# Two-layer hybrid encoder on one core: two raw weight chunks of the MLP's lead land in the tiles of the shared sums, one pair's squares are held back in both layers, and one hold is kept in one layer only

## The chip, the core and the metric

The kernel runs on one core of one Trainium2 chip. The metric is the time of one execution in microseconds (us), and less is better. Before the change three runs took 1929.17, 1929.80 and 1929.84 us, so the median is 1929.8 us. One further execution was recorded by the hardware profiler.

## The reference

A trunk of two layers over 256 tokens of width 2048. Each layer has a token mixer (neighbourhood attention in layer 0, grouped-query attention in layer 1) beside four cross-attention heads, an output projection, and a dense MLP with squared ReLU. What matters here is the end of the projection and the MLP behind it:

```
for i in range(DEPTH):                      # DEPTH = 2
    n = rms_norm(h, attn_norm[i])
    ...
    h = h + jnp.concatenate([mix, cross], axis=-1) @ w_o[i]
    n = rms_norm(h, mlp_norm[i])
    h = h + jnp.square(jax.nn.relu(n @ w_up[i])) @ w_down[i]
return rms_norm(h, final_norm)
```

`w_up[i]` is 2048 x 8192 and `w_down[i]` is 8192 x 2048, all in float32.

## The kernel before

**Products of split numbers.** Every float32 operand is split into a high part (a copy rounded to `float32r`, on ACT) and a low part (the number less its high part, on DVE); TensorE multiplies high by high, low by high and high by low. The helper `split` (L401 on ACT, L402 on DVE) does this for every 1 MB chunk of weights. So each chunk goes: a DMA issued by SP, an ACT copy, a DVE subtraction, and then the matmuls. Names ending in `h` and `l` are the parts: `uh`, `ul` of an up chunk, `bh`, `bl` and `th`, `tl` of a down chunk.

**The MLP.** One layer has 64 up chunks, numbered m (128 features each), and a down projection that is mostly a Strassen form of seven products instead of eight over pairs of up chunks. The first six up chunks (`LEAD`) run alone, and are called the lead here; then come 58 steps, numbered n. A step is: "first" (9 matmuls with `bh`/`bl`, lines L1103, L1105, L1106), one up chunk m = 6 + n (32 matmuls, L294 and L297, in two halves), and "second" (12 matmuls with `th`/`tl`, same lines as "first"). What remains is done by plain products. `squared` (from L1004) takes the sums of an up chunk out of PSUM (`u_y`, L1012 and L1013), applies ReLU and square (`c`, L1014 and L1015), and after every second chunk makes the seven left-hand matrices of that pair (DVE, L1023 to L1025) and splits them (`a_s`). Pair j is needed first by a "first" of step n = 2, 3, ... in an order given by `RUNS`; pair 2 (chunks 4 and 5, the last of the lead) is first used in step n = 2.

**Where the raw weights land.** An up chunk's raw weights land in one of two buffers (tag `U`, function `loaded`). The third and fourth up chunk (m = 2 and m = 3) thus wait until the splits of chunk 0 and chunk 1 have been made. The two tiles `z0` and `z1` (each 128 x 2048 float32, 1 MB) hold the four shared sums of the Strassen form; they are made at the beginning of the MLP, and their first write comes at the end of step n = 3. They belong to a pool (`mlp`) that takes the memory of the pools of the projection, which are closed at that point.

**Order.** Work is cut into grains in the order of TensorE. `run_all` walks the grains and calls each grain's load, preparation and run a number of grains ahead (the triple `ahead`); `later(n, fn)` puts off a function by n grains; a scheduler then places the instructions on each engine's queue, in which they run strictly in order. `past(fn, pair)` holds the instructions of `fn` behind the pair of instructions given (an ACT copy and a DVE subtraction). In both layers the splits of chunk m = 0 are held in this way behind the last split of the projection's weights (`box["weights"]`).

Of the kernel before, what the change touches and what calls it, by code (L numbers as in the profile page):

```python
# [38 lines left out]
LEAD = 6  # L39
# [66 lines left out]
def encoder_kernel(ctx: ExitStack, tc: tile.TileContext, t: dict, out: bass.AP):  # L106
    nc = tc.nc
# [58 lines left out]
    soon = {}  # L166
# [787 lines left out]
    def up_grains(layer, m):  # L954
        own = {}
        lead = m < LEAD

        def load():
            own["raw"] = loaded(t[f"w_up{layer}"][m], "U")

        def prep(hf):

            if m == 0:
                past(lambda: prepared(hf), box["weights"])
                return
            with tc.issue_after(box["summed"].ins) if m in (1, 2) else nullcontext():
                prepared(hf)

        def prepared(hf):
            half = 2 * m + hf  # L970
            if lead and (half in (2, 4) or half > 4 and half % 3 == 2):

                if half < 5:
                    room = at.side.tile([P, 2, HALF], F32R, tag="b", bufs=3, name="u_b")
                    own[hf] = room[:, 0], room[:, 1]
                else:
                    own[hf] = tuple(at.mlp.tile([P, CH], F32R, tag=x, name=f"u_{x}")[:, :HALF] for x in ("th", "tl"))
                box["splits"].append(split(*own[hf], own["raw"][:, hf * HALF : (hf + 1) * HALF]))
            else:
                own[hf] = half_of_side(own["raw"], hf)  # L980

        def run(hf):
            if m == hf == 0:
                closed("cat", "ring")
                at.mlp = opened("mlp")
                box["z"] = [at.mlp.tile([P, 4, 512], F32, tag=f"z{q}", name=f"z{q}") for q in range(2)]
                box["z_set"], box["back"] = set(), set()
            if hf == 0:
                if lead:
                    own["ps"] = at.acc.tile([P, 512], F32, tag="acc", name="ps_u")  # L990
                else:
                    own["ps"] = sum_of("up")

            with tc.issue_after(box["late"].ins) if m == hf == 0 else nullcontext():
                products_of_both(own["ps"], box["hT"], hf * (KT // 2), KT // 2, *own.pop(hf), keep_order=not lead)

        def after():
            squared(layer, m, own["ps"])

        soon = (8, 8, 3) if m == 1 else SOONER  # L1000
        return [Grain(lambda: run(0), None, load, None, lambda: prep(0), soon),
                Grain(lambda: run(1), after, None, None, lambda: prep(1), SOONER)]

    def squared(layer, m, ps):  # L1004

        e = m % 2
        if e == 0:
            box["c"] = at.mlp.tile([P, 8, P], F32, tag="c", bufs=2, name="c")
        c = box["c"]
        two = c[:, 2 * e : 2 * e + 2, :]  # L1010
        y = at.side.tile([P, SEQ], F32, tag="junk", bufs=1, name="u_y")
        nc.scalar.activation(y, ps[:, SEQ:], AF.Copy)  # L1012
        nc.vector.tensor_tensor(y, ps[:, :SEQ], y, op=ALU.add)  # L1013
        nc.scalar.activation(two, y.rearrange("p (i b) -> p b i", b=2), AF.Relu)  # L1014
        nc.scalar.activation(two, two, AF.Square)  # L1015
        if e == 0:
            return
        pair = m // 2
        if pair >= max(STEPPED):
            a = at.mlp.tile([P, 2, 4, P], F32R, tag="a", bufs=6, name="a_p")  # L1020
            split(a[:, 0], a[:, 1], c[:, :4])
        else:
            nc.vector.tensor_tensor(c[:, 4, :], c[:, 0, :], c[:, 2, :], op=ALU.subtract)  # L1023
            nc.vector.tensor_tensor(c[:, 5:7, :], c[:, 0:5:4, :], c[:, 1, None, :].to_broadcast([P, 2, P]), op=ALU.add)
            box["made"] = nc.vector.tensor_tensor(c[:, 7, :], c[:, 3, :], c[:, 6, :], op=ALU.subtract)  # L1025
            a = at.mlp.tile([P, 2, 7, P], F32R, tag="a", bufs=6, name="a_s")
            split(a[:, 0], a[:, 1], c[:, 1:])
            if pair >= min(STEPPED):

                n = pair - min(STEPPED)  # L1030
                if n == 0:
                    box["a_0"] = at.mlp.tile([P, max(STEPPED) - min(STEPPED), 2, P], F32R, tag="a", bufs=6, name="a_0")
                split(box["a_0"][:, n, 0], box["a_0"][:, n, 1], c[:, 0])
        box["a", pair] = a
        if m == UPS - 1 and layer == 1:
            later(2, load_gf)
# [11 lines left out]
    def down_grains(layer, n, begins, ends, sooner):  # L1048

        q, j = STEPS[n]  # L1050
        own = {}

        def load():
            own["b"] = at.side.tile([P, 4, 512], F32, tag="b", bufs=3, name="b")
            nc.sync.dma_start(own["b"].rearrange("p a b -> p (a b)"),
                              t[f"w_pair{layer}"][j * 2 + q])

        def behind(fn, far=4):

            return (lambda: past(fn, box["splits"][-far])) if n < 2 else fn  # L1060

        def pre():

            b, s = own["b"], at.side.tile([P, 4, 512], F32, tag="T", bufs=2, name="t")
            nc.scalar.activation(s[:, 3, :], b[:, 3, :], AF.Copy)  # L1065
            nc.gpsimd.dma_start(s[:, 3, :], b[:, 1, :], accum_op=ALU.add)  # L1066

            with ExitStack() as held:
                if n == 2:
                    held.enter_context(tc.issue_after(box["made"].ins))  # L1070
                if 0 < n < 4:
                    held.enter_context(tc.issue_after(box["bl"].ins))
                box["t3"] = nc.vector.tensor_tensor(s[:, 0, :], b[:, 3, :], b[:, 0, :], op=ALU.add)
            nc.vector.tensor_tensor(s[:, 1, :], s[:, 0, :], b[:, 1, :], op=ALU.add)
            nc.vector.tensor_tensor(s[:, 2, :], s[:, 1, :], b[:, 2, :], op=ALU.add)
            own["t"] = s

        def prep_first():
            own["first"] = tuple(at.mlp.tile([P, 3 * 512], F32R, tag=x, name=x) for x in ("bh", "bl"))
            b = own["b"][:, :3].rearrange("p a b -> p (a b)")  # L1080
            if sooner:

                with tc.issue_after(box["t3"].ins):
                    split(*own["first"], b)
            else:
                box["bl"] = split(*own["first"], b)[1]

        def prep_second():
            own["second"] = tuple(at.mlp.tile([P, CH], F32R, tag=x, name=x) for x in ("th", "tl"))
            split(*own["second"], own["t"].rearrange("p a b -> p (a b)"))  # L1090

        def run(which, products):
            if n == 0 and which == "first":
                open_strassen(layer)
            hi, lo = own.pop(which)
            a = box["a", j]
            for name, ai, bi in products:
                if begins and name not in box["back"]:
                    sum_of(name)
                start = begins and name not in box["back"]  # L1100
                ps = pairs(box["ps"][name])
                mh, ml = (in_turn(x[:, bi * 512 : (bi + 1) * 512]) for x in (hi, lo))
                ins = nc.tensor.matmul(ps, a[:, 0, ai, :], mh, start=start, stop=False, skip_group_check=True)  # L1103
                pin(ins)
                nc.tensor.matmul(ps, a[:, 0, ai, :], ml, start=False, stop=False, skip_group_check=True)  # L1105
                nc.tensor.matmul(ps, a[:, 1, ai, :], mh, start=False, stop=ends, skip_group_check=True)  # L1106
                if begins:
                    box["back"].discard(name)

        def after(products):  # L1110
            if ends:
                for name, _, _ in products:
                    taken(q, name, n == len(STEPS) - 1)

        def after_second():
            after(SECOND)
            if ends:
                box["z_set"].add(q)
            if ends and j == STEPPED[q] - 1:
                folded(q, n == len(STEPS) - 1)  # L1120

        return [Grain(lambda: run("first", FIRST), lambda: after(FIRST), load, behind(pre), behind(prep_first, 4 if n else 1),
                      (12, 8, 4) if sooner else (12, 5, 4)),
                Grain(lambda: run("second", SECOND), after_second, None, None, behind(prep_second), SOONER)]
# [541 lines left out]
```

## Time and profile before

| | before |
|---|---|
| median of three runs | 1929.8 us (1929.17 to 1929.84) |
| the profiled execution's own time | 1932.01 us |
| its span | 1930.2 us |
| mean granted TensorE clock | 0.996 |
| HBM read | 397.78 MB |

The profile is one execution. The engines are PE (matmuls), PEld (weight loads of PE), DVE, ACT, POOL and SP; SP issues nearly all of the DMAs. A row of the timeline gives the start, the duration, the engine, the line, the operation, the tile written and the tiles read, and in brackets how long the engine sat idle before it and what ended the wait. Layer 0's projection ends and its lead begins at about 403 us; in layer 1 this is at about 1285.6 us. The loop of 58 steps follows each of them.

### The profile page before, as it was taken

The page shows a single profiled execution, that of the slowest core. Times are in us where ns is not written, and L with a number is a line of the kernel's source. Part 1 is how long each engine was busy: PE and PEld are TensorE (multiplying, and loading weights), DVE is VectorE, ACT ScalarE, POOL GpSimd, SP SyncE. Part 2 cuts the span into 40 slices and gives each one's busy share as a digit, 9 for nine tenths or more (in the row PEclk, how much of TensorE's full clock was granted, in tenths as well). Part 3 has the DMA queues.
Part 4 walks back from the last instruction along what each step waited for, and adds up shares of the span by engine and source line. Part 5 has one row for each costly group of instructions (what it writes and reads, how often), then busy time and mean ns, then how long its engine had stood idle before and what let it go on. Part 6 is the DMA issues. An engine that isn't in the chain of part 4 may idle for free.

```text
span 1930.2 us, 27774 instructions
## 1 busy us (share of the span) xinstructions
PE 1904.5 (99%) x10278; PEld 1702.3 (88%) x10278; DVE 1740.6 (90%) x2226; ACT 1406.8 (73%) x2042; POOL 153.8 (8%) x191
## 2 busy tenths in 40 slices
PE   9999999999999999999999999999999999999998
PEld 9999989888888988888888888888888888888887
DVE  7888878589999999999999778888999999999997
ACT  6755555567787887878876658667777878878785
POOL 0000000000000000000011001000000000000010
PEclk9999999999999999999999999999999999999999
DMA  8965666666877888778777765667778788788784
GB/s 301 331 209 179 228 205 201 241 214 219 247 243 245 244 247 245 232 243 246 238 241 224 262 217 166 222 213 238 244 235 250 235 244 249 232 248 243 239 251 145
DMA packets 119048, 451.35 MB, mean 234 GB/s; under 512 B 24832, under 2 KB 50176, under 8 KB 71552
## 3 DMA queue, kind: packets, MB, share of 16 engines
q1 hardware_dynamic: 99168, 415.12, 62.9%
q0 software_dynamic: 19456, 33.93, 10.8%
q8 instruction: 81, 1.33, 0.3%
q10 hardware_dynamic: 288, 0.52, 0.1%
q14 instruction: 55, 0.45, 0.1%
HBM read 397.78 MB, written 4.19 MB: 208 GB/s over the span
## 4 chain that ended last, share of the span: by engine, by line
PE 83%; DVE 7%; DMA 4%; ACT 3%; issue 2%; SPq 1%; POOL 0%; DVEq 0%; POOLq 0%; ACTq 0%
PE ps_u L297 21%; PE ps_u L294 10%; PE p L1105 9%; PE p L1106 9%; PE p L1103 9%; PE ps_s L297 5%; PE ps_m L278 5%; PE ps_m L281 5%; PE ps_m L282 5%; PE ps_s L294 3%; DVE lo L402 1%; DMA raw_U<-in_w_up 1%; PE ps_s L307 1%; SPq L503 1%; DVE ul L402 1%
## 5 line engine op out<-in xcount | busy, mean ns | idle before, releaser
L297 PE MATMUL ps_u<-hT,uh 128*128 128x512 f32 x1968 | 651.4, 382 | 0.0
L294 PE MATMUL ps_u<-hT,ul 128*128 128x256 f32 x1968 | 537.1, 273 | 1.8 <-DVE ul L402 1.8
L297 PEld LDWEIGHTS ps_u<-hT,uh 128*128 128x128 f32 x1968 | 371.8, 189 | 51.4
L294 PEld LDWEIGHTS ps_u<-hT,ul 128*128 128x128 f32 x1968 | 377.6, 192 | 7.8 <-DVE ul L402 2.6
L402 DVE TENSOR_TENSOR ul<-raw_U,uh 128x1024 fp32r<-128x1024 f32 x262 | 318.3, 1217 | 10.8 <-ACT uh L401 10.7
L402 DVE TENSOR_TENSOR lo<-raw,hi 128x1024 fp32r<-128x1024 f32 (+1 forms) x220 | 260.2, 1193 | 53.6 <-ACT hi L401 53.2
L401 ACT ACTIVATE uh<-raw_U 128x1024 fp32r<-128x1024 f32 x262 | 276.4, 1056 | 22.1 <-PE ps_u L297 9.4
L402 DVE TENSOR_TENSOR tl<-t,th 128x2048 fp32r<-128x2048 f32 x116 | 265.4, 2288 | 29.3 <-ACT th L401 28.0
L401 ACT ACTIVATE hi<-raw 128x1024 fp32r<-128x1024 f32 (+1 forms) x220 | 225.0, 1034 | 84.1 <-PE ps_m L282 58.8
L401 ACT ACTIVATE th<-t 128x2048 fp32r<-128x2048 f32 x116 | 221.5, 1910 | 38.4 <-PE p L1106 38.4
L402 DVE TENSOR_TENSOR bl<-b,bh 128x1536 fp32r<-128x1536 f32 x116 | 203.1, 1751 | 0.9 <-ACT bh L401 0.9
L1066 POOL DMA_DIRECT2D t<-b x116 | 101.1, 871 | 1072.8 <-ACT t L1065 835.8
L1103 PE MATMUL p<-th,a_s 128*128 128x512 f32 x464 | 175.9, 379 | 0.0
L1105 PE MATMUL p<-tl,a_s 128*128 128x512 f32 x464 | 175.9, 379 | 0.0
L1106 PE MATMUL p<-th,a_s 128*128 128x512 f32 x464 | 175.9, 379 | 0.0
L401 ACT ACTIVATE bh<-b 128x1536 fp32r<-128x1536 f32 x116 | 172.1, 1483 | 0.0
L297 PE MATMUL ps_s<-nT,hi 128*128 128x512 f32 x448 | 148.6, 382 | 0.0
L1105 PE MATMUL p<-bl,a_s 128*128 128x512 f32 x348 | 133.4, 383 | 2.6 <-DVE bl L402 2.6
L1103 PE MATMUL p<-bh,a_s 128*128 128x512 f32 x348 | 133.1, 383 | 2.9 <-ACT bh L401 2.9
L1106 PE MATMUL p<-bh,a_s 128*128 128x512 f32 x348 | 133.2, 383 | 0.0
L1014 ACT ACTIVATE c<-u_y 128x256 f32<-128x256 f32 x128 | 67.3, 526 | 85.3 <-DVE u_y L1013 85.3
L294 PE MATMUL ps_s<-nT,lo 128*128 128x256 f32 x448 | 122.6, 274 | 0.0
(308 smaller groups left out, 3688.5 us busy)
## 6 DMA issues: line engine op xcount, KB each, us to landing
raw_U<-in_w_up SPq DMA_DIRECT2D x128, 1024.0 KB, 6.0
b<-in_w_pair SPq DMA_DIRECT2D x116, 1024.0 KB, 6.1
raw<-in_w_o SPq DMA_DIRECT2D x32, 1024.0 KB, 5.2
t<-b POOLq DMA_DIRECT2D x116, 256.0 KB, 7.0
raw<-in_w_b SPq DMA_DIRECT2D x21, 1024.0 KB, 5.5
raw<-in_w_av SPq DMA_DIRECT2D x12, 1024.0 KB, 5.2
raw<-in_w_aq SPq DMA_DIRECT2D x12, 1024.0 KB, 5.0
raw<-in_w_ak SPq DMA_DIRECT2D x12, 1024.0 KB, 5.0
```

What stands on the lines that cost most here:

```text
L278: first = nc.tensor.matmul(ps, ah, mh, start=st, stop=False)
L281: nc.tensor.matmul(ps, ah, ml, start=False, stop=False)
L282: final = nc.tensor.matmul(ps, al, mh, start=False, stop=sp)
L294: ins = nc.tensor.matmul(pairs(ps[:, :SEQ]), lo[:, s], x[:, 0], start=k == 0, stop=False, skip_group_check=True)
L297: nc.tensor.matmul(ps.rearrange("p (n i b) -> p n i b", n=2, b=2), hi[:, s], x, start=False, stop=k == KT - 1, skip_group_check=True)
L401: first = nc.scalar.activation(dst_hi, src, AF.Copy)
L402: return first, nc.vector.tensor_tensor(dst_lo, src, dst_hi.bitcast(F32), op=ALU.subtract)
L1014: nc.scalar.activation(two, y.rearrange("p (i b) -> p b i", b=2), AF.Relu)
L1066: nc.gpsimd.dma_start(s[:, 3, :], b[:, 1, :], accum_op=ALU.add)
L1103: ins = nc.tensor.matmul(ps, a[:, 0, ai, :], mh, start=start, stop=False, skip_group_check=True)
L1105: nc.tensor.matmul(ps, a[:, 0, ai, :], ml, start=False, stop=False, skip_group_check=True)
L1106: nc.tensor.matmul(ps, a[:, 1, ai, :], mh, start=False, stop=ends, skip_group_check=True)
```

## The change

Three edits, all in the MLP's code:

1. The raw weights of up chunks m = 2 and m = 3 land in `z0` and `z1` instead of the two `U` buffers. Their load is called one grain after the grain that makes those tiles. The `U` buffers so go to chunks 0, 1, 4, 5, 6, ...
2. The hold of chunk 0's splits behind the projection's last weight split stays in layer 1 and goes in layer 0.
3. `squared` is cut in two. For the last chunk of the lead (m = 5) the second part, `squares_of_pair` (ReLU, square, the pair's left-hand matrices and their split), is put off by three grains and held behind the split `bh`/`bl` of a down chunk (`box["b_split"]`, a new name for a pair that was there already). For every other chunk it runs as before.

```
         def load():
-            own["raw"] = loaded(t[f"w_up{layer}"][m], "U")
+            if m in (2, 3):
+                own["raw"] = box["z"][m - 2].rearrange("p a b -> p (a b)")
+                nc.sync.dma_start(own["raw"], t[f"w_up{layer}"][m])
+            else:
+                own["raw"] = loaded(t[f"w_up{layer}"][m], "U")
 
         def prep(hf):
 
-            if m == 0:
+            if layer and m == 0:
                 past(lambda: prepared(hf), box["weights"])
                 return
...
-        soon = (8, 8, 3) if m == 1 else SOONER
+        soon = (8, 8, 3) if m == 1 else (2 * m, 8, 4) if m in (2, 3) else SOONER
...
         nc.scalar.activation(y, ps[:, SEQ:], AF.Copy)
         nc.vector.tensor_tensor(y, ps[:, :SEQ], y, op=ALU.add)
+        if m == LEAD - 1:
+            later(3, lambda: past(lambda: squares_of_pair(layer, m, c, two, y), box["b_split"]))
+        else:
+            squares_of_pair(layer, m, c, two, y)
+
+    def squares_of_pair(layer, m, c, two, y):
+
         nc.scalar.activation(two, y.rearrange("p (i b) -> p b i", b=2), AF.Relu)
         nc.scalar.activation(two, two, AF.Square)
-        if e == 0:
+        if m % 2 == 0:
             return
...
-                box["bl"] = split(*own["first"], b)[1]
+                box["b_split"] = split(*own["first"], b)
+                box["bl"] = box["b_split"][1]
```

**What it moves on SP, layer 0.** These are SP's DMAs from the loads of up chunks 0 and 1 on, before the change; `raw` are the last chunks of the projection, `h_t` and `h_s` small copies of the activations, `raw_U` up chunks in their order m, `b` down chunks in their order n.

```order
L951 DMA raw_U<-in_w_up 128x2048 x2
L216 DMA raw<-in_w_o 128x2048 x8
L503 DMA h_t<-h_t 128x2x128 x8
L503 DMA h_s<-h_s 128x2x128 x4
L951 DMA raw_U<-in_w_up 128x2048
L1055 DMA b<-in_w_pair 128x2048
L951 DMA raw_U<-in_w_up 128x2048 x2
L1055 DMA b<-in_w_pair 128x2048 x2
L951 DMA raw_U<-in_w_up 128x2048 x3
```

And the same place with the change; the third `raw_U` is now chunk 4, the fourth chunk 5, and the two `z` are chunks 2 and 3.

```order
L951 DMA raw_U<-in_w_up 128x2048 x2
L216 DMA raw<-in_w_o 128x2048 x2
L951 DMA raw_U<-in_w_up 128x2048
L216 DMA raw<-in_w_o 128x2048 x6
L503 DMA h_t<-h_t 128x2x128 x8
L503 DMA h_s<-h_s 128x2x128 x4
L961 DMA z_4253<-in_w_up 128x2048
L961 DMA z_4254<-in_w_up 128x2048
L1066 DMA b<-in_w_pair 128x2048
L951 DMA raw_U<-in_w_up 128x2048
```

Chunk 4 has moved ahead of six loads of the projection, and chunks 2 and 3 are issued one behind the other, ahead of the first down chunk. The first `z` waits for the projection's last split on DVE; the fourth `raw_U` waits for the split of chunk 1's second half.

**What it moves on SP, layer 1.** The same queue in layer 1, from the small copies on, before the change; the three `raw_U` are chunks 2, 3 and 4.

```order
L503 DMA h_s<-h_s 128x2x128 x4
L951 DMA raw_U<-in_w_up 128x2048
L1055 DMA b<-in_w_pair 128x2048
L951 DMA raw_U<-in_w_up 128x2048
L1055 DMA b<-in_w_pair 128x2048
L951 DMA raw_U<-in_w_up 128x2048
```

With the change the first `raw_U` of the piece is chunk 4, and the second is chunk 5.

```order
L503 DMA h_s<-h_s 128x2x128 x4
L951 DMA raw_U<-in_w_up 128x2048
L961 DMA z_12539<-in_w_up 128x2048
L961 DMA z_12540<-in_w_up 128x2048
L1066 DMA b<-in_w_pair 128x2048
L951 DMA raw_U<-in_w_up 128x2048
```

Chunk 4 now stands where chunk 2 stood, and chunk 2 is issued behind it; here its load waits for the projection's last matmul on PE.

**What it moves on ACT, layer 0.** ACT's queue from the `u_y` of chunk 5 on, before the change: `t` belongs to the down chunk of n = 2, the two `c` and the `a_s` to pair 2, `bh` to n = 1, and `uh` to chunk 7.

```order
L1012 ACTIVATE u_y<-ps_u 128x256
L1065 ACTIVATE t<-b 128x512
L1014 ACTIVATE c<-u_y 128x256
L1015 ACTIVATE c<-c 128x256
L401 ACTIVATE a_s<-c 128x896
L401 ACTIVATE bh<-b 128x1536
L401 ACTIVATE uh<-raw_U 128x1024
```

And with the change.

```order
L1016 ACTIVATE u_y<-ps_u 128x256
L1076 ACTIVATE t<-b 128x512
L401 ACTIVATE bh<-b 128x1536
L1025 ACTIVATE c<-u_y 128x256
L1026 ACTIVATE c<-c 128x256
L401 ACTIVATE uh<-raw_U 128x1024
L1016 ACTIVATE u_y<-ps_u 128x256
L401 ACTIVATE uh<-raw_U 128x1024
L401 ACTIVATE a_s<-c 128x896
```

The `bh` of n = 1 has moved past the pair's three instructions, and `a_s` now comes behind both halves of chunk 7. DVE's queue moves in the same way: `bl` of n = 1 ahead of the pair's three `c`, and the pair's `a_s` just ahead of `tl` of n = 1. In layer 1 both queues move alike here.

## The prediction

> **What bounds the kernel now.** I read the page's busy times first, then the table of busy times by stretches of 20 us over the whole span, then the list of who waited for whom, and last the timelines of PE, ACT and DVE at the few places where PE waits.
>
> ```profile
> span 1930.2 us, 27774 instructions
> PE 1904.5 (99%) x10278; PEld 1702.3 (88%) x10278; DVE 1740.6 (90%) x2226; ACT 1406.8 (73%) x2042; POOL 153.8 (8%) x191
> 440.00:460.00 20.00, 16.59 (x83) 14.18 (x82) 16.44 (x24) 13.13 (x18) 0.89 (x1) 0.91 0.57 197
> 460.00:480.00 20.00, 20.00 (x110) 17.97 (x110) 19.81 (x23) 16.20 (x20) 1.74 (x2) 1.00 0.78 244
> 1320.00:1340.00 20.00, 17.89 (x88) 14.81 (x87) 16.58 (x24) 13.74 (x17) 0.86 (x1) 0.91 0.61 200
> ```
>
> PE is busy 1904.5 of 1930.2 us, so the whole kernel has some 26 us of idle PE. The columns of the stretches are the length, then the busy time (and count) of PE, PEld, DVE, ACT and POOL, the granted TensorE clock, and the DMA share and rate. In the loop (460 to 480) PE is busy all 20.00 us; DVE, at 19.81, follows it closely but does not hold it. The idle time that this change can reach stands in the lead and the first steps of each MLP. Most of it is in the two stretches 440 to 460 and 1320 to 1340, with PE at 16.59 and 17.89 of 20 us, and there the clock falls too, to 0.91 on average.
>
> ```profile
> PE p L1103 <- ACT bh L401: 2.9, 2, 2.1
> PE p L1105 <- DVE bl L402: 2.6, 2, 1.3
> ```
>
> These are the two of PE's waits (total us, times, longest) that stand behind those stretches. They are one place in each layer: the "first" of step n = 1, which waits for `bh` and then `bl`. Smaller waits stand in the lead, and their rows come with its terms.
>
> **The change part by part.**
>
> *The held pair (edit 3).* Here is PE around the "first" of n = 1, layer 0, then layer 1: the last matmul of the "second" before it, its first and second matmul, and the first matmul of the up chunk behind it.
>
> ```profile
> 447.75 0.38 PE L1106 MATMUL p<-th,a_s 128*128 128x512 f32 x1
> 450.22 0.48 PE L1103 MATMUL p<-bh,a_s 128*128 128x512 f32 x1 [2.10 <-ACT bh L401]
> 452.01 0.80 PE L1105 MATMUL p<-bl,a_s 128*128 128x512 f32 x1 [1.31 <-DVE bl L402]
> 455.46 0.27 PE L294 MATMUL ps_u<-hT,ul 128*128 128x256 f32 x1
> ...
> 1329.19 0.38 PE L1106 MATMUL p<-th,a_s 128*128 128x512 f32 x1
> 1330.37 0.48 PE L1103 MATMUL p<-bh,a_s 128*128 128x512 f32 x1 [0.80 <-ACT bh L401]
> 1332.16 0.48 PE L1105 MATMUL p<-bl,a_s 128*128 128x512 f32 x1 [1.31 <-DVE bl L402]
> 1335.56 0.56 PE L294 MATMUL ps_u<-hT,ul 128*128 128x256 f32 x1
> ```
>
> Such matmuls start 0.216 us apart when nothing waits (9 would take 1.94 us, from 0.216 behind the last "second"). Undisturbed, the up chunk would begin at 447.97 + 1.94 = 449.91 and at 1329.41 + 1.94 = 1331.35. So the place costs 455.46 - 449.91 = 5.55 us in layer 0 and 1335.56 - 1331.35 = 4.21 us in layer 1, waits and lowered clock together:
>
> ```profile
> 452.00:456.00 4.00, 3.98 (x12) 3.31 (x13) 4.00 (x6) 1.63 (x4) 0.00 (x0) 0.58 0.70 250
> 1280.00:1284.00 4.00, 3.26 (x15) 2.89 (x16) 4.00 (x5) 2.90 (x8) 0.00 (x0) 1.00 0.92 195
> ```
>
> The clock is 0.58 in the 4 us after the waits of layer 0 (in layer 1 the stretch of 20 us has the same mean, 0.91), which is some 1.7 us of each loss. A single wait of 1.3 us before 1281 left it at 1.00. What makes `bh` late is ACT's and DVE's queue:
>
> ```profile
> 444.23 0.63 ACT L1065 ACTIVATE t<-b 128x512 f32<-128x512 f32 x1 [0.95 <-DVE tl L402]
> 447.85 0.95 ACT L401 ACTIVATE a_s<-c 128x896 fp32r<-128x896 f32 x1 [1.20 <-DVE c L1025]
> 448.70 1.47 ACT L401 ACTIVATE bh<-b 128x1536 fp32r<-128x1536 f32 x1
> 441.91 2.29 DVE L402 TENSOR_TENSOR tl<-t,th 128x2048 fp32r<-128x2048 f32 x1
> 450.20 1.76 DVE L402 TENSOR_TENSOR bl<-b,bh 128x1536 fp32r<-128x1536 f32 x1 [0.28 <-ACT bh L401]
> ```
>
> Between `t` and `bh` stands pair 2, which passes from ACT to DVE, back and across again. With the pair held, `bh` follows `t` at about 444.8 and ends near 446.3; `bl` ends near 448.1, against PE's 447.97. That alone removes all but 0.2 us. Since the lead also gets earlier (below), I walk it from the moment P at which PE leaves the lead: `th` needs a tile that PE frees at P and takes 1.9, `tl` ends at P + 4.3, `t` at 4.9, `bh` at 6.4, `bl` at 8.2, while PE, after "first" (1.9), an up chunk (5.3) and "second" (2.6), asks for it at P + 9.8. The stall goes with 1.6 us to spare. Term: **5.5 + 4.2 = 9.7 us**.
>
> The pair is not gone. Its `c` and `a_s` (about 2 us of DVE) now stand between `bl` and `tl` of n = 1, and that `tl` is late next. By the same walk DVE has two `ul`, three `t`, two `u_y`, three `c` and the `a_s` there, 6.5 us, and `tl` ends at P + 16.9, while PE asks for it at P + 17.0. So this cover is thin. I bound the leftover by 0 below and by the pair's 2 us above in each layer, and take 0.5 each, nearer to the walk: **-1.0 us**. The pair itself is used in "first" of n = 2, at P + 19.6, 5 us behind its `a_s`.
>
> *The lead in layer 0 (edits 1 and 2).* PE's first matmul of chunk 0, then of chunk 1, the wait in its second half, the first of chunk 2, and the wait in chunk 5:
>
> ```profile
> 403.01 0.27 PE L294 MATMUL ps_u<-hT,ul 128*128 128x256 f32 x1
> 408.64 0.35 PE L294 MATMUL ps_u<-hT,u_b 128*128 128x256 f32 x1 [0.35 <-DVE u_b L402]
> 412.65 0.38 PE L294 MATMUL ps_u<-hT,ul 128*128 128x256 f32 x1 [0.89 <-DVE ul L402]
> 416.57 0.27 PE L294 MATMUL ps_u<-hT,u_b 128*128 128x256 f32 x1
> ...
> 432.84 0.38 PE L294 MATMUL ps_u<-hT,ul 128*128 128x256 f32 x1 [0.39 <-DVE ul L402]
> ```
>
> The chain of waits shows why chunk 1's `ul` is late: it stands on DVE behind chunk 2's two splits, and these wait for chunk 2's load, which waited for chunk 0's `ul`:
>
> ```profile
> 401.58 1.31 DVE ul L402
> ...
> 402.91 5.02 DMA raw_U<-in_w_up
> ...
> 410.33 1.13 DVE u_tl L402
> 411.46 1.14 DVE ul L402
> ...
> 419.98 10.40 DMA raw_U<-in_w_up
> ```
>
> With the change three things fall away. Chunk 0's two splits (2.4 us of DVE, 2.0 of ACT) are made in the projection, near 347. There ACT does one copy of 1.06 us each 2.59 and DVE one subtraction of 1.23, so both fit:
>
> ```profile
> 345.76 1.06 ACT L401 ACTIVATE hi<-raw 128x1024 fp32r<-128x1024 f32 x1 [1.53 <-PE ps_m L282]
> ```
>
> Chunk 2's load leaves when the projection's last split ends, near 400.7, not at 402.91, and lands near 406. And chunk 1's `ul` stands ahead of chunk 2's splits, so that it ends near 408.8, while PE wants it at 410.8. Matmul work from 403.01 to chunk 2 is 32 pairs of 0.328 us (10.5) and 8 transposes (1.2), so chunk 2 can begin at 414.8 instead of 416.57: 1.8 us. Chunk 5's raw weights, which landed at 419.98 + 10.40 = 430.38 (the last row above), are asked for near 409, and the 0.4 us goes too. Term: **2.2 us**, between 0.8 (chunk 2 lands 2 us later than I think) and 2.4.
>
> *The lead in layer 1.* Here the hold stays and chunk 2's load is issued later than before: chunk 4 takes its place at 1284.12, and `z0` waits for the projection's last matmul, near 1285.8.
>
> ```profile
> 1284.12 0.33 SPq L951 DMA_DIRECT2D raw_U<-in_w_up  x1
> 1289.33 1.06 ACT L401 ACTIVATE u_b<-raw_U 128x1024 fp32r<-128x1024 f32 x1 [2.36 <-DMA raw_U<-in_w_up]
> 1294.75 0.38 PE L294 MATMUL ps_u<-hT,ul 128*128 128x256 f32 x1 [0.53 <-DVE ul L402]
> ```
>
> A load alone took 5.2 us here. If chunk 2 shares the DMA engines with chunk 4 it lands between 1290.9 (alone) and 1292.5 (one whole megabyte behind it, at the 400 GB/s that DMA reaches when full). PE's wait of 0.53 for chunk 1's `ul` goes, because that `ul` no longer waits for chunk 2. But ACT's copies of the last activations stand behind chunk 2's `u_th`, and the last of them is ready some 4.9 us after the landing; PE wants it at 1297.4. Up to a landing at 1292.5 nothing is lost, then each us costs one. Term: **0.5 us**, between -1.5 and 0.9.
>
> [...]
>
> **Sum.** 9.7 - 1.0 + 2.2 + 0.5 = 11.4 us off the profiled execution's 1932.0 us (1930.2 of span), so 1920.6. The median of the runs is 1929.8, 2.2 less than the profiled one, and I take the same 11.4 off it: **1918.4 us**.
>
> **Rivals.**
>
> *The stall moves to `tl` or `bl` behind the pair.* If the walk is off by the pair's own 2 us and PE waits 2 us in each layer with the clock falling again, 2 x (2.0 + 1.7) replaces the 1.0: 1918.4 + 6.4 = 1924.8. For it speaks the thin cover of 0.1 us; against it that `bl` has 1.6 to spare and that a wait of 1.3 did not lower the clock. [...]
>
> *Chunk 2 lands late in layer 1*, by 3 us over my estimate: the 0.5 becomes -2.5 and the clock may fall (1.7). That is 1921.4 to 1923.1.
>
> *The held pair does not help*, because `bh` then waits for its raw `b` or for PE: only the lead's 2.7 us remain, 1927.1, which is within 0.2%. Against it: ACT never waited for `b` at this place, but for DVE.
>
> *Slower: the loop becomes bound by DVE.* DVE is busy 19.81 of 20 us. If the earlier entry shifts its phase so that each of the 58 steps loses 0.15 us in both layers, 2 x 58 x 0.15 = 17.4 us, less the 11.4 won, gives 1935.8. It decides where DVE's work for a step is over PE's 9.8 us. Against it: the queues differ only up to n = 3, and DVE still waits there.
>
> **Chances.** My forecast 0.58; stall moved 0.18; late chunk 0.07; no help 0.11; slower 0.06. Two runs can be told apart by about 0.2%, that is 3.9 us; faster means under 1925.9. Faster: 0.58 + 0.18 + 0.07, less 0.01 for the moved stall's tail, 0.82; same 0.12; slower 0.06. The range runs from 1916.5 (no leftover, clean leads: 1918.4 - 1.9) to 1925.0, with the moved stall in it; what lies outside is the 0.17 of the last two rivals.
>
> **What the new profile would show.** Right: no wait of PE for `bh` or `bl` above 0.3 us at the "first" of n = 1, a clock of 1.00 from 440 to 460 and from 1320 to 1340, chunk 2 of layer 0 beginning 11.8 us after chunk 0, and 20.00 us of PE in each loop stretch. Wrong: a new wait at the "second" of n = 1, PE waiting for activations near 1296, or a loop with PE below 20.00.

## The result

The changed kernel takes 1917.87 us (median of 4 runs, 1916.59 to 1918.79) against 1929.82 us before (4 runs, 1929.17 to 1930.95): a ratio of 0.9931, 95% interval 0.9918 to 0.9943. The forecast was 1918.4 us. Of the profiled executions, before took 1932.0 us and the changed kernel 1918.8 us.

The page of the changed kernel and its table of busy times by stretches, with the columns as before:

```profile
span 1916.9 us, 27770 instructions
PE 1898.6 (99%) x10278; PEld 1699.4 (89%) x10278; DVE 1739.9 (91%) x2226; ACT 1405.5 (73%) x2042; POOL 154.1 (8%) x191
440.00:460.00 20.00, 20.00 (x111) 18.00 (x110) 19.08 (x25) 16.09 (x20) 1.76 (x2) 1.00 0.66 202
460.00:480.00 20.00, 19.97 (x109) 17.55 (x108) 19.52 (x21) 16.09 (x22) 1.72 (x2) 1.00 0.74 224
1320.00:1340.00 20.00, 20.00 (x110) 17.98 (x109) 19.78 (x24) 15.62 (x19) 1.71 (x2) 1.00 0.74 227
```

PE was busy 16.59 and 17.89 us in the first and last of these stretches, and now is busy all 20, at a clock of 1.00. PE's waits by whom it waited for (total us, times, longest) no longer name `bh` or `bl`. What they still name in the lead is

```profile
PE ps_u L297 <- DVE hT L432: 1.0, 1, 1.0
PE ps_u L294 <- DVE u_b L402: 0.4, 1, 0.4
PE ps_u L294 <- ACT hT L431: 0.2, 1, 0.2
```

all three in layer 1. To see where the time went, the two traces are laid beside each other at matmuls that both have. These are PE's rows in the timeline of before (the first matmul of the up chunk of n = 0 and of n = 10, in each layer, and ahead of layer 1's the lead's first), and then those of the changed kernel: the lead's first matmul, chunk 2's first (layer 0), and the up chunks of n = 0, 1 and 10.

```profile
440.13 0.27 PE L294 MATMUL ps_u<-hT,ul 128*128 128x256 f32 x1
543.42 0.27 PE L294 MATMUL ps_u<-hT,ul 128*128 128x256 f32 x1
1285.59 0.27 PE L294 MATMUL ps_u<-hT,ul 128*128 128x256 f32 x1
1321.57 0.27 PE L294 MATMUL ps_u<-hT,ul 128*128 128x256 f32 x1
1424.07 0.27 PE L294 MATMUL ps_u<-hT,ul 128*128 128x256 f32 x1
```

```profile
402.54 0.27 PE L294 MATMUL ps_u<-hT,ul 128*128 128x256 f32 x1
414.15 0.27 PE L294 MATMUL ps_u<-hT,u_b 128*128 128x256 f32 x1
437.05 0.27 PE L294 MATMUL ps_u<-hT,ul 128*128 128x256 f32 x1
446.82 0.27 PE L294 MATMUL ps_u<-hT,ul 128*128 128x256 f32 x1
535.37 0.27 PE L294 MATMUL ps_u<-hT,ul 128*128 128x256 f32 x1
...
1275.51 0.27 PE L294 MATMUL ps_u<-hT,ul 128*128 128x256 f32 x1
1312.46 0.27 PE L294 MATMUL ps_u<-hT,ul 128*128 128x256 f32 x1
1322.24 0.27 PE L294 MATMUL ps_u<-hT,ul 128*128 128x256 f32 x1
1410.79 0.27 PE L294 MATMUL ps_u<-hT,ul 128*128 128x256 f32 x1
```

Differences of such rows (the other rows of before, 403.01, 455.46 and 1335.56, stand in the prediction) give this table of parts, in us, for all kernels of this study. "Lead" runs from its first matmul to the up chunk of n = 0, "n 0-1" from there to that of n = 1, "n 1-10" nine steps further (nine undisturbed steps of 9.77 take 88.0). Only before and the changed kernel have two profiles: the parts of before differ by up to 1 us between them, those of the changed kernel by 0.3 us.

| kernel | lead 0 | n 0-1 | n 1-10 | lead 1 | n 0-1 | n 1-10 | sum 0 | sum 1 | ratio to before, interval |
|---|---|---|---|---|---|---|---|---|---|
| before | 37.12 | 15.33 | 87.96 | 35.98 | 13.99 | 88.51 | 140.41 | 138.48 | 1 |
| before, again | 38.10 | 15.46 | 88.76 | 36.72 | 14.68 | 88.51 | 142.32 | 139.91 | 1 |
| changed | 34.51 | 9.77 | 88.55 | 36.95 | 9.78 | 88.55 | 132.83 | 135.28 | 0.9931 (0.9918 to 0.9943) |
| changed, again | 34.25 | 9.78 | 88.52 | 37.10 | 9.78 | 88.55 | 132.55 | 135.43 | 0.9953 (0.9940 to 0.9967) |
| hold_only | 36.83 | 10.89 | 88.95 | 35.99 | 10.62 | 88.97 | 136.67 | 135.58 | 0.9961 (0.9947 to 0.9975) |
| hold_z45 | 36.31 | 9.78 | 88.56 | 35.99 | 9.78 | 88.54 | 134.65 | 134.31 | 0.9947 (0.9930 to 0.9963) |
| lead_only | 34.26 | 12.96 | 88.56 | 36.55 | 12.96 | 88.57 | 135.78 | 138.08 | 0.9972 (0.9960 to 0.9983) |
| held_both | 37.05 | 9.77 | 88.50 | 37.16 | 9.78 | 88.45 | 135.32 | 135.39 | 0.9945 (0.9930 to 0.9960) |
| held_none | 34.38 | 9.77 | 88.55 | 34.90 | 11.04 | 88.13 | 132.70 | 134.07 | 0.9948 (0.9933 to 0.9963) |
| z_layer0 | 34.29 | 9.78 | 88.50 | 35.98 | 10.83 | 88.95 | 132.57 | 135.76 | 0.9944 (0.9929 to 0.9959) |
| c2_first | 34.59 | 9.77 | 88.56 | 35.20 | 10.74 | 88.95 | 132.92 | 134.89 | 0.9931 (0.9917 to 0.9946) |
| c2_pool | 34.26 | 11.67 | 88.52 | 35.20 | 12.97 | 88.51 | 134.45 | 136.68 | 0.9951 (0.9934 to 0.9967) |
| z67_plain | 34.48 | 9.77 | 88.46 | 36.77 | 9.77 | 88.52 | 132.71 | 135.06 | 0.9940 (0.9927 to 0.9952) |
| z67 | 34.27 | 9.77 | 88.51 | 35.20 | 9.77 | 88.51 | 132.55 | 133.48 | 0.9938 (0.9926 to 0.9951) |

The other 47 steps of each loop took 459.35 to 459.38 us in every one of these kernels. Between before and the changed kernel the two sums fall by 7.58 and 3.20 us, 10.8 together. The rest of the profiled difference (1930.2 - 1916.9 = 13.3 us) stands outside what was edited: 0.47 us ahead of the first lead and 2.03 us between the layers.

### The profile page after: what moved, and what is told of

Read it like the earlier page. It is cut to its first block, busy times and chain, and to the rows that moved or that the text cites. A ratio compares the mean times of both kernels' runs of the same rounds, so it can differ in the third digit from the quotient of the medians.

```text
span 1916.9 us, 27770 instructions
## 1 busy us (share of the span) xinstructions
PE 1898.6 (99%) x10278; PEld 1699.4 (89%) x10278; DVE 1739.9 (91%) x2226; ACT 1405.5 (73%) x2042; POOL 154.1 (8%) x191
## 4 chain that ended last, share of the span: by engine, by line
PE 87%; DVE 5%; DMA 2%; ACT 2%; issue 2%; SPq 1%; POOL 0%; DVEq 0%; POOLq 0%; ACTq 0%
PE ps_u L297 23%; PE ps_u L294 12%; PE p L1117 9%; PE p L1118 9%; PE p L1115 9%; PE ps_s L297 6%; PE ps_m L281 5%; PE ps_m L282 5%; PE ps_m L278 4%; PE ps_s L294 3%; DVE lo L402 2%; PE ps_s L307 1%; SPq L503 1%; DVE sc_t L518 1%; ACT b_y L1424 0%
```

## The experiments

**The kernel before, a second time** (no edit). It was to tell whether those 2.03 us belong to the change.

> The kernel before, unchanged, recorded a second time. In the two profiles the stretch between the layers (from the loop of layer 0 to the lead of layer 1) differs by 2.03 us (up chunk starts: 8.05 us earlier in the last step of layer 0, 10.08 us earlier at the lead of layer 1), and no edit touches it. If that is a difference between executions and not the change, this profile may show the lead of layer 1 about 2 us earlier than 1285.59 (near 1283.5) with no clock drop near 1185; if it belongs to the kernel before, the lead begins again at 1285.6 with the drop. In both cases the 'first' of n = 1 waits for bh and bl again, and the up chunks of n = 0 and n = 1 stand 15.3 us (layer 0) and 14.0 us (layer 1) apart.

Between the layers it took 281.46 us, where the first profile of before had 282.81 and the two of the changed kernel 280.78 and 280.66. So most of the 2.03 us (1.35) is a difference between executions: the first profile had a mean clock of 0.72 from 1184 to 1188 us, in the attention of layer 1, and this one 1.00. The leads differ by about 1 us in the same way, and the one run took 1933.22 us. At n = 1 of layer 1 this profile shows more. PE's rows there, and the stretches:

```profile
1331.56 0.48 PE L1103 MATMUL p<-bh,a_s 128*128 128x512 f32 x1 [1.50 <-ACT bh L401]
1333.35 0.48 PE L1105 MATMUL p<-bl,a_s 128*128 128x512 f32 x1 [1.31 <-DVE bl L402]
1336.75 0.38 PE L294 MATMUL ps_u<-hT,ul 128*128 128x256 f32 x1 [1.41 <-DVE u_y L1013]
```

```profile
1328.00:1332.00 4.00, 2.50 (x11) 1.66 (x9) 2.56 (x5) 2.82 (x3) 0.27 (x1) 1.00 0.38 66
1332.00:1336.00 4.00, 2.04 (x9) 1.43 (x8) 3.97 (x5) 1.67 (x3) 0.00 (x0) 1.00 0.41 109
```

The waits are longer than in the first profile (0.80 and 1.31), and this time the clock stays at 1.00. The place still costs 14.68 - 9.77 = 4.9 us, because PE now waits 1.41 us for `u_y`, which in the first profile the slow clock had covered. DVE was 3.97 us busy in those 4, and set the time. How much the lowered clock cost in the first profile is told by DVE's rows for that `u_y`, in layer 0 and in layer 1:

```profile
454.22 0.41 DVE L1013 TENSOR_TENSOR u_y<-ps_u,u_y 128x256 f32<-128x256 f32 x1
1335.09 0.42 DVE L1013 TENSOR_TENSOR u_y<-ps_u,u_y 128x256 f32<-128x256 f32 x1
```

In layer 1 it ended at 1335.51 and PE's up chunk began at 1335.56: the lowered clock was no cost of its own there. In layer 0 it ended at 454.63 and the up chunk began at 455.46, so that at most 0.8 us were the clock's.

**Only the held pair.** Edit 3 as in the change, the rest as before.

```
         def load():
             own["raw"] = loaded(t[f"w_up{layer}"][m], "U")
...
+        if m == LEAD - 1:
+            later(3, lambda: past(lambda: squares_of_pair(layer, m, c, two, y), box["b_split"]))
+        else:
+            squares_of_pair(layer, m, c, two, y)
...
```

> Only the held pair (edit 3); the raw weights land and chunk 0 is held as before. Theory (bh of n = 1 is late because it stands behind pair 2 on ACT's and DVE's queues): no wait of PE for bh or bl, up chunks n = 0 and n = 1 9.8 us apart in both layers, clock 1.00 in the stretches, less 0 to 1 us of ripple: 1929.8 - 9.8 + 0.6 = about 1920.6 us. Rival (bh waits for its raw weights or for PE to free its tile): the distances stay at 15.3 and 14.0 us and the time at 1929.8. Rival (the stall only moves to tl of n = 1 or bl of n = 2): a new wait of about 2 us there, and 1925.

The waits for `bh` and `bl` are gone in both layers, so their cause, the queue behind pair 2, holds, and the first rival falls. But n = 0 to n = 1 takes 10.89 and 10.62 us, not 9.8, and the time is 1923.72 us (5 runs; before 1931.49 in the same comparison), 0.9961. A new wait has come, as the second rival said, though at another place and half as long. ACT, DVE and PE in layer 0, from their timelines:

```profile
428.83 1.06 ACT L401 ACTIVATE uh<-raw_U 128x1024 fp32r<-128x1024 f32 x1 [3.67 <-DMA raw_U<-in_w_up]
429.93 1.22 DVE L402 TENSOR_TENSOR ul<-raw_U,uh 128x1024 fp32r<-128x1024 f32 x1 [4.34 <-ACT uh L401]
449.39 0.38 PE L294 MATMUL ps_u<-hT,ul 128*128 128x256 f32 x1 [0.94 <-DVE u_y L1013]
```

Chunk 5's raw weights land late, DVE idles 4.34 us in the lead, and 20 us later it is behind: PE waits until DVE's `u_y` has emptied the sums of the up chunk before. In layer 1 DVE's longest idle time of the lead is 1.96 us, and PE waits some 0.6 us for `u_y`. That the landing is the cause is not shown by these rows; the run after the next one tests it.

**Only edits 1 and 2.** The pair is not held.

```
-        if m == LEAD - 1:
-            later(3, lambda: past(lambda: squares_of_pair(layer, m, c, two, y), box["b_split"]))
-        else:
-            squares_of_pair(layer, m, c, two, y)
+        squares_of_pair(layer, m, c, two, y)
```

> Edits 1 and 2 without the held pair. Theory (the two places add up): the lead of layer 0 is 2.6 us shorter, that of layer 1 1.0 us longer, as in the changed kernel's profile, and the 'first' of n = 1 keeps its waits: 1929.8 - 1.6 = about 1928.2 us, the distances of the up chunks n = 0 and n = 1 still near 15 and 14 us. Rival (the earlier landings of chunks 4 and 5 let ACT and DVE get ahead, so that the wait for bh shrinks by itself): distances of 12 us or less, and 1925 us or less.

The leads are as in the changed kernel, and n = 0 to n = 1 falls to 12.96 us in both layers, without a held pair: neither the theory's 15 and 14 nor the rival's 12. The time is 1925.29 us (6 runs), 0.9972. PE in layer 0:

```profile
444.52 0.48 PE L1112 MATMUL p<-bh,a_s 128*128 128x512 f32 x1 [0.50 <-ACT bh L401]
446.32 0.48 PE L1114 MATMUL p<-bl,a_s 128*128 128x512 f32 x1 [1.31 <-DVE bl L402]
448.99 0.38 PE L294 MATMUL ps_u<-hT,ul 128*128 128x256 f32 x1 [0.68 <-DVE u_y L1017]
```

The wait for `bh` has shrunk from 2.10 to 0.50 us. So the two parts are not independent: both the queue and the late landing of the lead's last chunks made this place cost 5.55 and 4.21 us, and either alone leaves a part of it.

**The held pair, and chunks 4 and 5 early.** This gives the held pair the early landing in another way, with the leads as before. The edit against the kernel with the held pair alone:

```
-            own["raw"] = loaded(t[f"w_up{layer}"][m], "U")
+            if m in (4, 5):
+                own["raw"] = box["z"][m % 2].rearrange("p a b -> p (a b)")
+                nc.sync.dma_start(own["raw"], t[f"w_up{layer}"][m])
+            else:
+                own["raw"] = loaded(t[f"w_up{layer}"][m], "U")
```

> Only the held pair, and in both layers the raw weights of chunks 4 and 5 (in place of 2 and 3) land in z0 and z1; chunk 0 is held as before. With the held pair alone, PE still waited 0.94 us in layer 0 and some 0.6 us in layer 1 for u_y at n = 1, and n = 0 to n = 1 took 10.89 and 10.62 us, n = 1 to n = 10 88.95 and 88.97 us; there DVE had idled 4.34 us in the lead of layer 0 behind ACT's 3.67 us wait for chunk 5's landing. Theory (that late landing shifts DVE's work behind PE's, and this is the edits' share in the place of n = 1): with chunk 5 early, 9.8 us and 88.5 us in both layers, while the two leads stay near 36.8 and 36.0 us; about 2.8 us less than the held pair alone. Rival (the wait for u_y comes from the held pair's work on DVE itself): 10.6 us or more and 88.9 us stay.

The theory's numbers came: 9.78 us in both layers, 88.56 and 88.54, with leads of 36.31 and 35.99. The time is 1920.18 us (4 runs), 0.9947. There is no wait for `u_y` left, so the late landing was what made it. PE at n = 0 and n = 1, both layers:

```profile
438.50 0.27 PE L294 MATMUL ps_u<-hT,ul 128*128 128x256 f32 x1
448.28 0.27 PE L294 MATMUL ps_u<-hT,ul 128*128 128x256 f32 x1
...
1313.59 0.27 PE L294 MATMUL ps_u<-hT,ul 128*128 128x256 f32 x1
1323.37 0.27 PE L294 MATMUL ps_u<-hT,ul 128*128 128x256 f32 x1
```

**Chunk 2 first in layer 1.** The changed kernel with one order added.

```
-                own["raw"] = loaded(t[f"w_up{layer}"][m], "U")
+                with tc.issue_after(box["z_in"].ins) if layer and m == 4 else nullcontext():
+                    own["raw"] = loaded(t[f"w_up{layer}"][m], "U")
...
```

> The changed kernel, with chunk 4's load in layer 1 issued behind those of chunks 2 and 3. Theory (chunk 4's load ahead of chunk 2's delays chunk 2, which lands 7.7 us after its issue, and the last activations behind its splits make PE wait 1.02 and 0.20 us): chunk 2 lands some 5.2 us after its issue, these two waits go, the lead of layer 1 from its first matmul to the up chunk of n = 0 is 1.2 us shorter (36.95 to about 35.7 us), and the time 1917.9 - 1.2 = 1916.7 us. Rival (chunk 2 is late for another reason, its wait for the projection's last matmul, or the load of chunk 3 beside it): 36.9 us stays and 1917.9.

In the changed kernel, SP issued chunk 4 and then chunks 2 and 3, and ACT waited for chunk 2 (the first row's `raw_U` is chunk 4):

```profile
1274.03 0.33 SPq L951 DMA_DIRECT2D raw_U<-in_w_up  x1
1275.71 0.81 SPq L961 DMA_DIRECT2D z<-in_w_up  x2
1283.42 1.06 ACT L401 ACTIVATE u_b<-z 128x1024 fp32r<-128x1024 f32 x1 [3.02 <-DMA z<-in_w_up]
```

With chunk 2 first, and then what ACT and PE waited for later:

```profile
1276.45 0.81 SPq L961 DMA_DIRECT2D z<-in_w_up  x2
1281.38 1.06 ACT L401 ACTIVATE u_b<-z 128x1024 fp32r<-128x1024 f32 x1 [0.23 <-DMA z<-in_w_up]
...
1306.75 1.06 ACT L401 ACTIVATE uh<-raw_U 128x1024 fp32r<-128x1024 f32 x1 [2.08 <-DMA raw_U<-in_w_up]
1322.19 0.38 PE L294 MATMUL ps_u<-hT,ul 128*128 128x256 f32 x1 [0.56 <-DVE u_y L1018]
```

Chunk 2 lands 4.9 us after its issue and not 7.7, and the lead is 1.75 us shorter (35.20). The theory holds for the lead. But 0.96 and 0.40 us are lost again at n = 1 and behind it, where DVE is late as above; here it is chunk 6 that landed late. The two sums of parts differ by 0.3 us from the changed kernel's, and the time, 1918.49 us, by nothing that can be told.

**Edit 1 in layer 0 only.**

```
-            if m in (2, 3):
+            if m in (2, 3) and not layer:
...
```

> The changed kernel with edit 1 in layer 0 only: in layer 1 the raw weights land as before. Theory (from the lead on, DVE cannot follow a PE that comes earlier without the early landing of chunk 4, so what the lead of layer 1 wins is given back at n = 1 and n = 2): in layer 1 the lead takes 36.0 us to the up chunk of n = 0, the step to n = 1 10.6 us with a wait for u_y, n = 1 to n = 10 89.0 us, together 135.6 us against 135.3 of the changed kernel: 1918.2 us. Rival (the terms of the lead and of n = 1 simply add): 36.0 + 9.8 + 88.5 = 134.3 us and 1916.9 us.

The theory's numbers came: 35.98, 10.83 and 88.95 us, 135.76 against 135.28. What the old landing wins in layer 1's lead it loses at n = 1 and behind it. The time was 1920.50 us, where the theory had 1918.2; the stretch between the layers was 283.82 us in this profile, 3 us over the changed kernel's, so that the time of itself says little.

**Chunk 0 held in both layers, and in neither.** The first takes edit 2 back, the second extends it to layer 1.

```
-            if layer and m == 0:
+            if m == 0:
```

> The changed kernel without edit 2: chunk 0 is held in layer 0 as well. Theory (in layer 0 edit 2 is what lets chunk 2's load leave ahead of chunk 4's and clears DVE for chunk 1): the lead of layer 0 becomes like that of layer 1, 36.5 to 37 us to the up chunk of n = 0 against 34.5, and the time about 1920 us. Rival (the landing in z alone does it, and the hold costs nothing): 34.5 us and 1917.9 us.

Layer 0's lead becomes 37.05 us, as the theory said: edit 2 is worth 2.5 us there. The time is 1920.79 us (4 runs), 0.9945. The trace shows the order on SP behind it: with the hold, chunk 4 is issued 0.38 us ahead of chunk 2, and PE waits 0.99 us for `hT` behind chunk 2's splits. That the order alone makes all of the 2.5 us was not tried in layer 0.

```
-            if layer and m == 0:
-                past(lambda: prepared(hf), box["weights"])
-                return
```

> The changed kernel with no hold of chunk 0 in either layer. Theory (DVE is full at the end of layer 1's projection, 20.00 of 20 us, so that chunk 0's 2.4 us of splits delay the projection's last splits, and a shorter lead is given back to DVE at n = 1): the lead of layer 1 near 34.6 us, but 0.5 to 2 us more before it, and 10 us or more from n = 0 to n = 1; the time 1917 to 1919 us. Rival (layer 1 behaves like layer 0): the whole gain of the lead, 2.4 us, stays and the time is 1915.5 us.

Layer 1's lead falls to 34.90 us, but the projection ahead of it pays. PE's waits for the projection's low parts are now

```profile
1254.87 0.48 PE L281 MATMUL ps_m<-lo,cat 128*128 128x512 f32 x1 [1.66 <-DVE lo L402]
1272.98 0.71 PE L281 MATMUL ps_m<-lo,cat 128*128 128x512 f32 x1 [2.30 <-DVE lo L402]
```

and 6.2 us in all against 2.9; from the loop of layer 0 to the lead of layer 1 it took 285.70 us against 280.78. That is 4.9 us more, over the theory's 0.5 to 2; up to 3 us of it can be a difference between executions, and the clock fell there too (mean 0.64 from 1272 to 1276). The time, 1921.65 us (4 runs), 0.9948, lies above the theory's 1917 to 1919. As the theory said, `u_y` is waited for again at n = 1 (11.04 us). The parts speak for the hold in layer 1; in the times it isn't shown, as the changed kernel itself had 0.9931 and 0.9953.

**The pair's three sums on POOL**, on top of chunk 2 first.

```
+            by = nc.gpsimd if m == LEAD - 1 else nc.vector
-            nc.vector.tensor_tensor(c[:, 4, :], c[:, 0, :], c[:, 2, :], op=ALU.subtract)
+            by.tensor_tensor(c[:, 4, :], c[:, 0, :], c[:, 2, :], op=ALU.subtract)
...
```

> The kernel with chunk 2 first in layer 1, and pair 2's three sums (the c of its left-hand matrices, 1.0 us of DVE in each layer) on POOL in place of DVE. Theory (after the lead DVE's backlog is the bound: PE waits for u_y because DVE has more work than PE between the lead and n = 1): in layer 1 the step from n = 0 to n = 1 falls from 10.74 to 9.8 us, and n = 1 to n = 10 from 88.95 to 88.5 us or less; in layer 0 the 0.6 us of ripple shrinks; about 1917 us. Rival (PE waits there for a landing of raw weights or for ACT): 10.7 and 88.95 us stay, 1918.5 us. If POOL is slow and a_s comes late, a new wait for a_s stands at the 'first' of n = 2.

This failed and tells neither theory apart. POOL, ACT, DVE and PE at n = 1 of layer 1:

```profile
1323.45 1.31 POOL L1038 TENSOR_TENSOR c<-c 128x128 f32<-128x128 f32 x1
1324.79 0.95 ACT L401 ACTIVATE a_s<-c 128x896 fp32r<-128x896 f32 x1 [2.88 <-POOL c L1038]
1322.70 1.75 DVE L402 TENSOR_TENSOR ul<-raw_U,uh 128x1024 fp32r<-128x1024 f32 x1
1327.26 0.38 PE L294 MATMUL ps_u<-hT,ul 128*128 128x256 f32 x1 [2.92 <-DVE u_y L1018]
```

ACT waits 2.88 us for POOL's last sum, and DVE's `u_y` stands behind the pair's `a_s` on DVE's queue, so PE waits 2.92 us. The time is 1923.01 us (4 runs), 0.9951.

**The changed kernel again, and chunks 6 and 7 early.** Two kernels let chunks 6 and 7 land in `z0` and `z1` as well, one on top of chunk 2 first, one on the changed kernel as it is.

```
-            if m in (2, 3):
-                own["raw"] = box["z"][m - 2].rearrange("p a b -> p (a b)")
+            if m in (2, 3, 6, 7):
+                own["raw"] = box["z"][m % 2].rearrange("p a b -> p (a b)")
...
```

> The changed kernel itself, recorded again beside the next two. If the table of parts is a property of the kernel, it repeats: lead of layer 0 34.5 us, n = 0 to n = 1 9.8 us in both layers, n = 1 to n = 10 88.5 us, lead of layer 1 36.9 us, all within 0.3 us. What lies between the layers (280.8 us) differed by up to 3 us between kernels in which nothing there was edited, and may differ again; then the time of a single profile says little below 2 us.

> The kernel with chunk 2 first in layer 1, and in both layers the raw weights of chunks 6 and 7 also land in z0 and z1, so that they leave earlier. In the kernel with chunk 2 first, ACT waited 2.08 us for chunk 6's landing, DVE 1.16 us for that, and PE 0.56 us for u_y at n = 1. Theory (that late landing is what took back the gain of the lead): no wait for u_y, n = 0 to n = 1 in layer 1 falls from 10.74 to 9.8 us, n = 1 to n = 10 from 88.95 to 88.5 us, the lead stays at 35.2 us: 1.4 us less than with chunk 2 first, 1.7 less than the changed kernel. Rival (DVE has more work than PE between the lead and n = 1 whatever lands when): 10.7 and 88.95 us stay.

> The changed kernel with the raw weights of chunks 6 and 7 in z0 and z1 too, and chunk 4 still ahead of chunk 2 in layer 1. ACT did not wait for chunk 6 in the changed kernel, so the lead of layer 1 stays at 36.9 us, n = 0 to n = 1 at 9.8 us, and the time is that of the changed kernel within 0.5 us. Theory on the ripple (DVE's backlog of pair 2, not a landing): n = 1 to n = 10 stays at 88.5 us. Rival (the ripple comes from late raw weights): 88.0 us in both layers, 1 us less in all.

The changed kernel's parts repeat within 0.3 us, while its time in this comparison was 1920.83 us (5 runs) against 1930.56: 0.9953, where the first comparison gave 0.9931. With chunk 2 first and chunks 6 and 7 early, ACT does not wait for chunk 6 and PE not at n = 1:

```profile
1303.95 1.05 ACT L401 ACTIVATE uh<-z 128x1024 fp32r<-128x1024 f32 x1
```

and the parts of layer 1 are 35.20, 9.77 and 88.51 us: the late landing was what took the lead's gain back, as in the theory. The sum of parts is 2.1 us below the changed kernel's (132.55 + 133.48 against 132.83 + 135.28), the best of the study, and the time is 1917.60 us (5 runs), 0.9938; the intervals of the two ratios overlap, so that a gain over the changed kernel in the time itself isn't shown. Without chunk 2 first nothing moves by more than the executions differ (1918.49 us, 5 runs), and n = 1 to n = 10 stays at 88.5 us: late raw weights of chunks 6 and 7 do not make that last ripple of 0.5 us.

## Why the prediction came out right, by its steps

*The place of n = 1.* The size was right: 5.56 and 4.21 us gone, 9.77 against 9.7. The step "That alone removes all but 0.2 us" was wrong. The held pair alone removes 4.44 and 3.37 us, 7.8 together; the other 2.0 come from the early landing of chunks 4 and 5, by which DVE no longer idles 4.34 us at one place in layer 0's lead (1.04 at most). The prediction walked the queues from the end of the lead as if DVE stood ready there. In the changed kernel it does. PE's first matmul after the lead in layer 0, and DVE's `bl` and `tl` of n = 1:

```profile
435.11 0.38 PE L1115 MATMUL p<-bh,a_s 128*128 128x512 f32 x1
```

```profile
441.62 1.76 DVE L402 TENSOR_TENSOR bl<-b,bh 128x1536 fp32r<-128x1536 f32 x1 [0.67 <-ACT bh L401]
449.57 2.29 DVE L402 TENSOR_TENSOR tl<-t,th 128x2048 fp32r<-128x2048 f32 x1
```

`bl` ended 8.3 us and `tl` 16.8 us after PE left the lead, where the walk had 8.2 and 16.9. The reading that the lowered clock is some 1.7 us of each loss was wrong: DVE's `u_y` left it none of the loss in layer 1 and at most 0.8 us in layer 0.

*The leftover.* Predicted as 1.0 us at `tl` of n = 1; measured against the first profile of before as 0.59 us in layer 0 and 0.04 in layer 1, and none of it at n = 1. In the changed kernel it lies between the up chunks of n = 3 and n = 6, in both layers. DVE's `tl` of n = 3 in layer 0, and PE's first matmul with it:

```profile
469.67 2.29 DVE L402 TENSOR_TENSOR tl<-t,th 128x2048 fp32r<-128x2048 f32 x1
472.01 0.48 PE L1117 MATMUL p<-tl,a_s 128*128 128x512 f32 x1
```

`tl` ends at 471.96, just before PE can start; in the same way `u_y` ends at 486.35 and the up chunk of n = 5 starts at 486.41. So a `tl` does come late, but two steps behind the one that the walk named. And it is not the held pair's price: the kernel without the held pair loses nearly as much there (88.56 and 88.57 from n = 1 to n = 10), at the same two places. In before, layer 0 ran these steps undisturbed in both profiles, and layer 1 lost 0.3 and 0.5 us there. (The 88.76 of the second profile is another loss, 0.8 us in the up chunk of n = 1, where the clock was still lowered: mean 0.82 from 456 to 460.) What in DVE's queue makes the ripple was not tried.

*The lead in layer 0.* Predicted 2.2, measured 2.6 us (37.12 to 34.51). Chunk 2 begins 414.15 - 402.54 = 11.6 us after chunk 0, predicted 11.8, before 13.6. With edit 2 taken back 2.5 us of it go.

*The lead in layer 1.* Predicted a gain of 0.5 (between -1.5 and 0.9), measured a loss of 0.97 us. The step that failed is the landing. The forecast put chunk 2's landing between 5.1 and 6.7 us after 1285.8; it came 7.6 us after its issue (ACT starts on it at 7.7), that is 0.9 us behind the forecast's latest. PE's wait for chunk 1's `ul` went as forecast (0.53), and 0.20 and 1.02 us for the last activations took its place; PE also asked for the last of them 11.2 us into the lead, where the walk had 1297.4 - 1285.6 = 11.8. That chunk 2 is late because it stands behind chunk 4 is shown by the run that turns the two around (4.9 us). The loads of this place landed in the order of their issue: chunk 4 at 1279.0, chunk 2 at 1283.3, chunk 3 at 1285.8 and the down chunk behind them at 1288.3. But the order alone does not give the size. Chunk 4 had been issued 1.7 us earlier and had landed at 1279.0; one megabyte more, at the 400 GB/s that the prediction used, would be there near 1281.6, and chunk 2 landed at 1283.3. The kernel before moved that much from 1066 to 1070 us, with its DMA at a share of 1.01 (the last two columns):

```profile
1066.00:1070.00 4.00, 4.00 (x20) 3.50 (x19) 2.42 (x8) 1.76 (x3) 0.00 (x0) 1.00 1.01 400
```

At the start of the time between the two landings the DMA of the changed kernel moved less (266 GB/s, the last column):

```profile
1278.00:1280.00 2.00, 1.94 (x16) 1.59 (x14) 2.00 (x5) 1.14 (x2) 0.00 (x0) 1.00 0.78 266
```

Why is open. The kernel before has two loads issued 0.4 us apart: that of an up chunk at 1293.59 and that of a down chunk at 1293.97 landed 4.9 and 7.0 us after their issue, 2.5 us apart.

*The rivals.* Chunk 2's late landing in layer 1, given 0.07, came in about half its size: 1.5 us off the term, not 3, and the clock did not fall. Waits of PE at n = 1 behind the pair came only where the landing was late (0.94 us), not in the changed kernel. The loop did not become bound by DVE: 459.36 us for its last 47 steps in both. The total came out well partly by luck, since errors met: the three places and the leftover sum to 10.8 us, not 11.4; lead 1 was 1.5 us worse than its term, lead 0 and the leftover 0.8 better, and outside the edits the profiled pair differs by 2.5 us, which at least in part is no gain of the change.

*The signs and the range.* No wait for `bh` or `bl`, a clock of 1.00 and chunk 2's start all came as named. Two of the signs of being wrong came as well, both small: the waits for activations in layer 1's lead, and PE at 19.97 of 20 us from 460 to 480. The lower end of the range, "1918.4 - 1.9", is not the sum of its parts: no leftover and clean leads give 1.0 + 0.2 + 0.4 = 1.6 us.

## What to carry to other kernels

A wait of the bound engine that is removed at one place has to be followed on the helper engines both ways: ahead, to what comes next in their queues, and back, to where they last idled, for a helper that idled 4 us for a late load was behind 20 us later here. Buffers that are free until later in the kernel are good landing places, but the load that is needed first is best issued first: here ACT could begin on chunk 2 4.9 us after its issue ahead of chunk 4, and 7.7 us after it behind chunk 4. Where executions differ by 2 us, distances between the same matmuls in two traces can tell apart what the time cannot; they too should be taken twice, as those of before differed by up to 1 us.

## What was not expected of the hardware

In the kernel before, the clock fell in one execution and not in the other, at the same place, n = 1 of layer 1: after waits of 0.80 and 1.31 us it fell (0.91 over 20 us), after 1.50, 1.31 and 1.41 us it did not (1.00 over the same 20 us). So the length of these waits alone does not decide it; what does was not shown.

POOL's three sums took from 1.06 to 1.31 us, where DVE takes 0.28 to 0.42, and while they ran a DVE subtraction that otherwise takes 1.22 us took 1.75. So while POOL did this work DVE lost time as well, 0.53 us in that row.
